# A two-layer decoder trunk on one core: the modulation rows' weights fetched one background step ahead of their sums

## The chip, the core and the metric

The kernel runs on one core of a Trainium2 chip. The core has a matrix engine (TensorE, in the profile PE, with its weight loads as PEld), VectorE (DVE), ScalarE (ACT), GpSimd (POOL) and SyncE (SP, which here only issues transfers). The engines run their own instruction streams and meet at semaphores. The metric is the device time of one execution in microseconds (us); a run's time is that of its slowest core, and there is one core here.

## What is computed

The reference is a trunk of two layers over a sequence of 512 tokens with 1024 channels. Each layer takes six modulation rows of 1024 numbers from the conditioning vector `c`, and uses them around a token mixer and a mixture of experts:

```python
ada_in = jax.nn.silu(c)
for i in range(DEPTH):
    mod = (ada_in @ w_ada[i] + b_ada[i]).reshape(b, 6, d)
    sh_m, sc_m, g_m = ...   # rows 0, 1, 2
    sh_f, sc_f, g_f = ...   # rows 3, 4, 5
    hm = rmsnorm(x, norm_mix[i]) * (1 + sc_m) + sh_m
    y = dilated_mixer(hm, ...) if i % 2 == 0 else forgetting_mixer(hm, ...)
    x = x + g_m * y
    hf = rmsnorm(x, norm_ffn[i]) * (1 + sc_f) + sh_f
    x = x + g_f * hierarchical_moe(hf, ...)
```

Layer 0 uses the dilated mixer ("mixer A": one projection to 9216 columns, three groups of attention with 16 heads each, merged by their denominators, and an out-projection). Layer 1 uses the forgetting mixer ("mixer B"). There are 16 experts per layer, all of them evaluated.

## The kernel before

The program is written in a tile framework: at build time a scheduler takes the operations in the order in which the code emits them, the free buffers of each pool and its own costs, and fixes from them one order of instructions for each engine. So a change of where the code emits something can move instructions on every engine.

**The background rows.** The first two rows of layer 0 are made at the start, in `begin`. The other ten are made by `ada` (L383 to L418), a generator of which `background` (L1324) makes ten, called jobs here. Each job needs 4 MB of weights, in eight pieces of 128 x 1024 numbers (512 KB): piece `kt` is fetched by SP into a tile of the tag `raw` (L393), and VectorE adds it to the accumulator with one scalar_tensor_tensor, `acc = piece * csil[kt] + acc` (L394; "a sum" below). Then the accumulator, which has 128 partial rows, is rounded to a high part `hi` on ScalarE (L399), a low part `nlo` is taken on VectorE (L400), and four TensorE matmuls with a column of ones add up the 128 partitions (L406 for the high part, L409 for the low). The row is evicted (L413 or L415) and stored (L416). There is one accumulator, one `nrow` and one `nlo`, so that the jobs follow one another.

**The weave.** `weave` (L227) runs the main work of mixer A and calls `next` on the front job once in two of its steps: a step of the main work is, for instance, a few projection matmuls. So the ten jobs are spread over mixer A, 12 calls to a job. The main work here is the projection (`part`, L295, L296 and L298: high times high, low times high, high times low) and attention: `qn`, the normed queries and keys, comes from VectorE (L470), is transposed on TensorE (L657, L658) and evicted into `qt` by ScalarE (L661) and into `kt` by VectorE (L662). The logits come from TensorE (L683 or L692), VectorE adds the bias (L691, the custom instruction), ScalarE takes the exponential (L693), TensorE transposes the result `nl` (L702), which VectorE or ScalarE evicts as `pt` (L209, L207), and L722 multiplies it with the values. `qn` and `nl` are transposed into banks of the same PSUM tag, so an eviction of `kt` also gives a bank back to L702.

**Buffers.** The tag `raw` has four buffers. The stream of projection weights (`Stream`, L107) holds up to three of them during mixer A, and the background job has what is left; the high part of its row (L398) sits there too. `row` has two buffers, which `nrow` and `nlo` hold during the jobs. When the last job is through, the row `g_m` of layer 0 is fetched into one of them (L606), and VectorE multiplies the weights of the out-projection with it (L149).

Of the kernel before, what the change touches and what calls it, by code (L numbers as in the profile page):

```python
# [20 lines left out]
KT = D // P  # L21
# [156 lines left out]
class Trunk:  # L178
# [205 lines left out]
    def ada(self, layer, j, norm, put):  # L384

        nc, i = self.nc, self.i
        acc = self.w.tile([P, D], F32, name="acc", tag="acc", bufs=1)
        row = self.nrow
        nc.gpsimd.memset(acc, 0.0)
        nc.gpsimd.dma_start(out=acc[0:1, :], in_=i["b_ada"][layer:layer + 1, j * D:(j + 1) * D])  # L390
        for kt in range(KT):
            raw = self.w.tile([P, 1024], F32, name="ada", tag="raw", bufs=4)
            nc.sync.dma_start(out=raw, in_=i["w_ada"][layer, kt * P:(kt + 1) * P, j * D:(j + 1) * D])  # L393
            nc.vector.scalar_tensor_tensor(acc, raw, self.csil[:, kt:kt + 1], acc, op0=OP.mult, op1=OP.add)  # L394
            if norm is not None and kt == KT // 2:
                nc.sync.dma_start(out=row, in_=self.bcast(norm, D, 1))
            yield
        hi, lo = self.w.tile([P, 1024], F32R, name="ada", tag="raw", bufs=4), self.nlo  # L398
        nc.scalar.activation(hi, acc, AF.Copy)  # L399
        nc.vector.tensor_tensor(lo, acc, hi.bitcast(F32), op=OP.subtract)  # L400
        for _ in range(3):
            yield
        ts = [self.bank("s")[0:1, :], self.bank("s")[0:1, :]]
        for h in range(2):
            cs = slice(h * 512, (h + 1) * 512)
            nc.tensor.matmul(ts[h], lhsT=self.one, rhs=hi[:, cs], start=True, stop=False)  # L406
        for h in range(2):
            cs = slice(h * 512, (h + 1) * 512)
            nc.tensor.matmul(ts[h], lhsT=self.one, rhs=lo[:, cs], start=False, stop=True)  # L409
        for h in range(2):  # L410
            cs = slice(h * 512, (h + 1) * 512)
            if norm is not None:
                nc.vector.scalar_tensor_tensor(row[:, cs], ts[h], 1.0, row[:, cs], op0=OP.add, op1=OP.mult)  # L413
            else:
                nc.scalar.activation(row[:, cs], ts[h], AF.Copy)  # L415
        nc.scalar.dma_start(out=put, in_=row)  # L416
        if (layer, j) == (0, 2):
            self.g_m = self.load_row(layer, 2)  # L418
# [986 lines left out]
```

## Time and profile before

| | us |
|---|---|
| median of 3 runs (1465.14, 1470.24, 1475.07) | 1470.24 |
| the profiled execution | 1476.0 |
| its span in the profile | 1474.2 |
| TensorE busy in it (matmuls) | 1328.8 (90%) |
| VectorE busy | 966.6 (66%) |
| ScalarE busy | 652.1 (44%) |
| the ten jobs' sums, L394, VectorE busy | 111.9 (80 instructions) |
| idle VectorE time just before them | 112.5 |

The profile gives busy times of each engine, a table of waits (which line of which engine stood idle, and whose work ended that), and the trace of single instructions with their start, length and, in brackets, the idle time ahead of each on its engine with what ended it. PEclk is the clock that TensorE was granted, as a share of its full 2.4 GHz.

### The profile page before, as it was taken

Reading aid. Unit: us, or ns where it says so; the run is one execution under the profiler, and the core shown is the slowest. Engines: PE = TensorE matmul, PEld = TensorE weight load, DVE = VectorE, ACT = ScalarE, POOL = GpSimd, SP = SyncE. Lnnn points to the kernel's source line nnn. Section 1 sums busy time; section 2 is a strip of 40 time slices with the busy share of each in tenths; the row PEclk is TensorE's granted clock in tenths of the full one; section 3 lists DMA queues with packets and bytes.
Section 4 is the critical chain, followed back from the end, with each engine's and each line's share of the span. In section 5 each row is a group of like instructions: output and inputs, shape, how many; then the busy total and the mean of one; then the engine's idle time right before and its main releaser. Section 6 shows DMA issues by size and latency. Waiting matters only on the chain. (4 is left out here: it accounts for less than half of the span.)

```text
span 1474.2 us, 20070 instructions
## 1 busy us (share of the span) xinstructions
PE 1328.8 (90%) x7017; PEld 1075.1 (73%) x7017; DVE 966.6 (66%) x1841; ACT 652.1 (44%) x1356; POOL 294.9 (20%) x192
## 2 busy tenths in 40 slices
PE   5799999989998999999969998499999999799995
PEld 3688888868986988887756665268888878566663
DVE  6775766675666675664677775376766753877772
ACT  6333544344433453344245554344544542355551
POOL 2312111221121211110232221211111100332221
PEclk9899999999999999999979999799999999889998
DMA  9356444644454645254679998604222463799981
GB/s 358 117 174 203 143 138 139 192 124 153 145 156 158 188 131 176 68 187 132 232 257 302 283 294 253 179 17 123 72 66 86 133 197 125 253 293 311 306 279 24
DMA packets 187156, 264.15 MB, mean 179 GB/s; under 512 B 23064, under 2 KB 148696, under 8 KB 187046
## 3 DMA queue, kind: packets, MB, share of 16 engines
q1 hardware_dynamic: 160742, 227.86, 47.5%
q0 software_dynamic: 8576, 16.85, 4.9%
q10 hardware_dynamic: 17728, 18.05, 4.1%
q8 instruction: 59, 0.97, 0.3%
q14 instruction: 51, 0.42, 0.1%
HBM read 249.85 MB, written 25.43 MB: 187 GB/s over the span
## 5 line engine op out<-in xcount | busy, mean ns | idle before, releaser
L295 PE MATMUL ps_pj<-hi,h 128*128 128x512 f32 (+1 forms) x1016 | 395.5, 398 | 6.2 <-ACT h L455 3.3
L296 PE MATMUL ps_pj<-lo,h 128*128 128x512 f32 (+1 forms) x1016 | 375.6, 378 | 0.8 <-POOL lo L153 0.8
L298 PE MATMUL ps_pj<-hi,h 128*128 128x512 f32 (+1 forms) x1016 | 290.0, 375 | 5.5 <-POOL h L380 5.4
L153 POOL TENSOR_TENSOR lo<-raw,hi 128x1024 fp32r<-128x1024 f32 x56 | 139.9, 2498 | 620.3 <-ACT hi L150 567.2
L295 PEld LDWEIGHTS ps_pj<-hi,h 128*128 128x128 f32 x1016 | 239.7, 236 | 31.5 <-issue 6.6
L296 PEld LDWEIGHTS ps_pj<-lo,h 128*128 128x128 f32 x1016 | 241.1, 237 | 16.6 <-POOL lo L153 1.4
L298 PEld LDWEIGHTS ps_pj<-hi,h 128*128 128x128 f32 x1016 | 212.1, 236 | 27.3 <-POOL h L380 7.8
L394 DVE SCALAR_TENSOR_TENSOR acc<-ada,csil,acc 128x1024 f32<-128x1024 f32 x80 | 111.9, 1399 | 112.5 <-DMA ada<-in_w_ada 112.2
L150 ACT ACTIVATE hi<-raw 128x1024 fp32r<-128x1024 f32 x126 | 132.2, 1051 | 100.0 <-PE ps_pj L298 52.1
L153 DVE TENSOR_TENSOR lo<-raw,hi 128x1024 fp32r<-128x1024 f32 x70 | 102.8, 1471 | 33.0 <-ACT hi L150 30.0
L295 PE MATMUL ps_pj<-hi,xh 128*112 128x512 f32 x256 | 105.4, 412 | 0.0
L296 PE MATMUL ps_pj<-lo,xh 128*112 128x512 f32 x256 | 104.0, 406 | 0.0
L298 PE MATMUL ps_pj<-hi,xl 128*112 128x512 f32 x256 | 80.9, 397 | 0.0
L1237 DVE SCALAR_TENSOR_TENSOR y<-ps_s,r_ws,g_f 112x512 f32<-112x512 f32 x64 | 47.9, 748 | 35.0 <-PE ps_s L1236 35.0
L455 ACT ACTIVATE xh<-ps_t 128x448 fp32r<-128x448 f32 x64 | 31.8, 542 | 84.3 <-PE ps_t L450 84.3
L462 ACT ACTIVATE sq<-ps_pj 128x512 f32<-128x512 f32 x63 | 37.0, 589 | 61.8 <-PE ps_pj L298 50.9
L927 DVE CUSTOM_DVE_ANT_0 nl<-ps_s,cums 128x128 f32<-128x128 f32 (+1 forms) x64 | 31.0, 484 | 46.5 <-PE ps_s L925 43.4
L153 DVE TENSOR_TENSOR lo<-h,hi 128x1024 fp32r<-128x1024 f32 x42 | 51.1, 1223 | 15.6 <-ACT hi L150 14.7
L722 PEld LDWEIGHTS ps_o<-vr,pt 128*128 128x128 f32 x480 | 58.0, 192 | 1.4
L929 ACT ACTIVATE nl<-nl,mn 128x128 f32<-128x128 f32 (+1 forms) x64 | 35.8, 559 | 50.6 <-DVE mn L927 50.0
L722 PE MATMUL ps_o<-vr,pt 128*128 128x64 f32 x480 | 57.3, 271 | 0.0
L464 DVE TENSOR_REDUCE qss<-sq 128x8 f32<-128x512 f32 x64 | 43.4, 679 | 20.0 <-ACT sq L462 19.7
(283 smaller groups left out, 2306.7 us busy)
## 6 DMA issues: line engine op xcount, KB each, us to landing
ada<-in_w_ada SPq DMA_DIRECT2D x85, 512.0 KB
raw<-in_a_w_in SPq DMA_DIRECT2D x128, 256.0 KB
h<-in_w_gate SPq DMA_DIRECT2D x42, 256.0 KB
h<-in_w_up SPq DMA_DIRECT2D x42, 256.0 KB
mix<-in_w_gate SPq DMA_DIRECT2D x37, 256.0 KB
mix<-in_w_up SPq DMA_DIRECT2D x37, 256.0 KB
raw<-in_w_down SPq DMA_DIRECT2D x18, 512.0 KB
h<-in_w_down SPq DMA_DIRECT2D x18, 512.0 KB
```

Source lines behind the costliest of these rows:

```text
L150: t.act = nc.scalar.activation(h, r, AF.Copy)
L153: eng.tensor_tensor(l, r, h.bitcast(F32), op=OP.subtract)
L295: nc.tensor.matmul(out, lhsT=hi, rhs=wh, start=first and n == 0, stop=False)
L296: nc.tensor.matmul(out, lhsT=hi, rhs=wl, start=False, stop=False)
L298: nc.tensor.matmul(out, lhsT=lo, rhs=wh, start=False, stop=last and n == len(terms) - 1)
L394: nc.vector.scalar_tensor_tensor(acc, raw, self.csil[:, kt:kt + 1], acc, op0=OP.mult, op1=OP.add)
L455: self.nc.scalar.activation(hv, tv, AF.Copy)
L462: nc.scalar.activation(sq, ps, AF.Square)
L464: nc.vector.tensor_reduce(ss, sq.rearrange("p (h d) -> p h d", d=HD), axis=AX.X, op=OP.add)
L722: nc.tensor.matmul(held["o"][:, at:at + HD], lhsT=pt[:, a * P:(a + 1) * P], rhs=v, start=(m == 0), stop=(m == len(terms) - 1))
L929: nc.scalar.activation(pr[:, sl], pr[:, sl], AF.Exp, scale=-1.0, bias=mn, accum_out=held["d"][:, h * 4 + b:h * 4 + b + 1])
L1237: nc.vector.scalar_tensor_tensor(y[:, cs], yp, m["ws"][0:CAP, e:e + 1], m["g_f"][0:CAP, cs], op0=OP.mult, op1=OP.mult)
```

## The change

The load of piece `kt + 1` is emitted right behind the sum of piece `kt`, ahead of the `yield`, and the first piece is fetched in a step of its own. A job then takes 13 calls of `next` in place of 12. No buffer is added, and each sum, cast and matmul is as before. In the changed kernel all lines from the load on have other numbers: the load is L394, the sum L401, the cast L408, the low part L409, the matmuls L415 and L418, and any line behind them is the old one plus 9 (L662 becomes L671, L691 L700, L149 stays).

```diff
--- before.py
+++ after.py
@@ -388,10 +388,19 @@
         row = self.nrow
         nc.gpsimd.memset(acc, 0.0)
         nc.gpsimd.dma_start(out=acc[0:1, :], in_=i["b_ada"][layer:layer + 1, j * D:(j + 1) * D])
-        for kt in range(KT):
+
+        def load(kt):
             raw = self.w.tile([P, 1024], F32, name="ada", tag="raw", bufs=4)
             nc.sync.dma_start(out=raw, in_=i["w_ada"][layer, kt * P:(kt + 1) * P, j * D:(j + 1) * D])
+            return raw
+
+
+        raw = load(0)
+        yield
+        for kt in range(KT):
             nc.vector.scalar_tensor_tensor(acc, raw, self.csil[:, kt:kt + 1], acc, op0=OP.mult, op1=OP.add)
+            if kt + 1 < KT:
+                raw = load(kt + 1)
             if norm is not None and kt == KT // 2:
                 nc.sync.dma_start(out=row, in_=self.bcast(norm, D, 1))
             yield
```

What the scheduler makes of it: the order on TensorE and VectorE is the same up to the end of the first job, and again from the end of mixer A's last projection to the end of the program. Between the two it differs on all engines. Three places follow. In these rows a wait is named by the semaphore of the engine or transfer queue that it waits on (DVE, Activation, PE, DMAHW); the number behind a tile's name is its number in the program.

**The fifth job.** SP in the kernel before, where the fifth job (accumulator `acc_2202`) fetches its last pieces:

```order
L114 DMA raw_2314<-in_a_w_in 128x4x256 [waits DMAHW3_49,DVE_49]
L114 DMA raw_2345<-in_a_w_in 128x2x256 [waits DMAHW4_49,DMAHW0_49,DVE_49]
L114 DMA raw_2345<-in_a_w_in 128x2x256 [waits DMAHW5_49]
L393 DMA ada_2348<-in_w_ada 128x1024 [waits DMAHW1_49,DVE_49]
L114 DMA raw_2361<-in_a_w_in 128x2x256 [waits DMAHW2_49,DVE_49]
L114 DMA raw_2361<-in_a_w_in 128x2x256
L114 DMA raw_2374<-in_a_w_in 128x2x256 [waits DMAHW3_49,Pool_49]
L114 DMA raw_2374<-in_a_w_in 128x2x256
L393 DMA ada_2377<-in_w_ada 128x1024 [waits DMAHW6_49,DVE_49]
```

SP in the changed kernel, the same job:

```order
L394 DMA ada_2364<-in_w_ada 128x1024 [waits DMAHW2_49,DVE_49]
L394 DMA ada_2385<-in_w_ada 128x1024 [waits DMAHW7_49,DMAHW0_49,DVE_49]
L394 DMA ada_2400<-in_w_ada 128x1024 [waits DMAHW1_49,DMAHW0_49,DVE_49]
L394 DMA ada_2455<-in_w_ada 128x1024 [waits DMAHW1_49,DVE_49]
L394 DMA ada_2470<-in_w_ada 128x1024 [waits DMAHW3_49,DMAHW2_49,DVE_49]
L114 DMA raw_2624<-in_a_w_in 128x2x256 [waits DMAHW4_49,DVE_49]
```

In both, a load of a piece waits for VectorE; the last five loads of this job, with weight loads among them before, now stand in a row. TensorE in the kernel before, around the same job's four matmuls (`ada_2398` is the high part):

```order
L657 MATMUL ps_t_2540<-J_417,qn_2449 128x128 [waits DVE_49,Activation_49]
L658 MATMUL ps_t_2540<-ident_87,qn_2449 128x128
L657 MATMUL ps_t_2540<-J_417,qn_2449 128x128
L406 MATMUL ps_s_2476<-ada_2398,one_99 1x512 [waits Activation_49]
L406 MATMUL ps_s_2477<-ada_2398,one_99 1x512
L658 MATMUL ps_t_2540<-ident_87,qn_2449 128x128
L295 MATMUL ps_pj_2533<-hi_2148,h_75 128x512
L296 MATMUL ps_pj_2533<-lo_2149,h_75 128x512
L295 MATMUL ps_pj_2533<-hi_2148,h_75 128x512
L409 MATMUL ps_s_2476<-nlo_443,one_99 1x512 [waits DVE_49]
L409 MATMUL ps_s_2477<-nlo_443,one_99 1x512
```

And in the changed kernel (`ada_2553` is the high part):

```order
L295 MATMUL ps_pj_2730<-hi_2356,h_79 128x256
L296 MATMUL ps_pj_2730<-lo_2357,h_79 128x256
L295 MATMUL ps_pj_2730<-hi_2356,h_79 128x256
L296 MATMUL ps_pj_2730<-lo_2357,h_79 128x256
L298 MATMUL ps_pj_2730<-hi_2356,h_78 128x256 x2
L298 MATMUL ps_pj_2730<-hi_2356,h_80 128x256 x2
L415 MATMUL ps_s_2762<-ada_2553,one_99 1x512 [waits PE_49]
L415 MATMUL ps_s_2763<-ada_2553,one_99 1x512 [waits DVE_49,PE_49]
L418 MATMUL ps_s_2762<-nlo_443,one_99 1x512
L418 MATMUL ps_s_2763<-nlo_443,one_99 1x512
```

Before, the first L406 waits for ScalarE's cast and stands between two transposes of `qn_2449`; now L415 stands behind the whole group of projection matmuls into `ps_pj_2730` and has no wait on ScalarE left.

**A `kt` in the eighth job.** VectorE in the kernel before, around one write of `kt` (L662) that gives a bank back to L702:

```order
L394 SCALAR_TENSOR_TENSOR acc_3922<-ada_4034,csil_109,acc_3922 128x1024 [waits DMAHW3_49]
L691 ISA nl_4088,st_3785<-ps_s_4074,bias_3783 128x256 [waits PE_49]
L691 ISA st_3785 128x1
L691 ISA nl_4088,st_3785<-ps_s_4074,bias_3783 128x256
L691 ISA st_3785 128x1
L464 TENSOR_REDUCE qss_4111<-sq_4109 128x8 [waits Activation_49]
L662 TENSOR_SCALAR kt_3752<-ps_t_4136,gains_419 128x2x128 [waits Activation_49]
```

And the write at the same place of the projection in the changed kernel (L671):

```order
L209 COPY pt_4042<-ps_t_4041 128x512 [waits PE_49]
L700 ISA nl_4058,st_3766<-ps_s_4048,bias_3764 128x256 [waits PE_49]
L700 ISA st_3766 128x1
L700 ISA nl_4058,st_3766<-ps_s_4048,bias_3764 128x256
L700 ISA st_3766 128x1
L700 ISA nl_4063,st_3766<-ps_s_4049,bias_3764 128x256 [waits PE_49]
L700 ISA st_3766 128x1
L700 ISA nl_4063,st_3766<-ps_s_4049,bias_3764 128x256
L700 ISA st_3766 128x1
L401 SCALAR_TENSOR_TENSOR acc_3722<-ada_4010,csil_109,acc_3722 128x1024 [waits DMAHW6_49,DVE_49]
L473 TENSOR_REDUCE qss_4084<-sq_4082 128x8 [waits Activation_49]
L671 TENSOR_SCALAR kt_3730<-ps_t_4109,gains_419 128x2x128 [waits Activation_49]
```

The sum stood ahead of the second pair of logits and now stands between the logits and `kt`, with one reduction between.

**The end of the last job.** VectorE in the kernel before, from the last `kt` of the projection on; the sums and `nlo` of the last job stand 22 rows and more ahead of this:

```order
L662 TENSOR_SCALAR kt_4314<-ps_t_5004,gains_419 128x2x128 [waits Activation_49]
L153 TENSOR_TENSOR lo_5039<-raw_4876,hi_5038 128x1024 [waits Activation_49]
L153 TENSOR_TENSOR lo_5082<-raw_4902,hi_5081 128x1024 [waits DMAHW3_49,Activation_49]
L149 TENSOR_TENSOR raw_5073<-raw_5073,row_1659 128x1024 [waits DMAHW2_49,DMAHW0_49,DVE_49]
L149 TENSOR_TENSOR raw_5085<-raw_5085,row_1659 128x1024 [waits DMAHW3_49,DMAHW1_49,Pool_49]
L149 TENSOR_TENSOR raw_5097<-raw_5097,row_1659 128x1024 [waits DMAHW4_49,DVE_49]
L149 TENSOR_TENSOR raw_5341<-raw_5341,row_1659 128x1024 [waits DMAHW5_49,DMAHW0_49,Pool_49]
L691 ISA nl_5143,st_5132<-ps_s_5133,bias_5130 128x256 [waits PE_49]
```

And in the changed kernel:

```order
L401 SCALAR_TENSOR_TENSOR acc_4801<-ada_4940,csil_109,acc_4801 128x1024 [waits DMAHW2_49,DVE_49]
L153 TENSOR_TENSOR lo_5027<-raw_4851,hi_5026 128x1024 [waits Activation_49]
L153 TENSOR_TENSOR lo_5073<-raw_4880,hi_5072 128x1024 [waits DMAHW4_49,Activation_49]
L401 SCALAR_TENSOR_TENSOR acc_4801<-ada_4962,csil_109,acc_4801 128x1024 [waits DMAHW3_49,DVE_49]
L401 SCALAR_TENSOR_TENSOR acc_4801<-ada_4977,csil_109,acc_4801 128x1024 [waits DMAHW4_49,DVE_49]
L401 SCALAR_TENSOR_TENSOR acc_4801<-ada_5002,csil_109,acc_4801 128x1024 [waits DMAHW5_49,DVE_49]
L409 TENSOR_TENSOR nlo_443<-acc_4801,ada_5063 128x1024 [waits Activation_49]
L700 ISA nl_5143,st_5132<-ps_s_5133,bias_5130 128x256 [waits PE_49]
L700 ISA st_5132 128x1
L700 ISA nl_5143,st_5132<-ps_s_5133,bias_5130 128x256
L700 ISA st_5132 128x1
L149 TENSOR_TENSOR raw_5061<-raw_5061,row_1781 128x1024 [waits DMAHW7_49,DMAHW3_49]
```

The last job's five last sums moved behind the merge of the attention groups, three of them into adjacent rows; L149 (which multiplies with the row that is fetched when this job is through) stood ahead of the logits of the block and now stands between them.

## Rows read from the trace of the kernel before

**Rows 1.** Busy times by stretch: busy us of each engine (instructions), clock, DMA share, GB/s.

```profile
65.00:660.00 595.00, 557.09 (x3085) 501.45 (x3083) 390.43 (x762) 249.22 (x609) 106.99 (x58) 0.97 0.49 153
257.60:261.00 3.40, 3.40 (x9) 1.88 (x10) 3.40 (x8) 2.43 (x4) 1.44 (x2) 0.50 0.62 175
261.00:264.40 3.40, 3.40 (x17) 3.33 (x16) 2.09 (x5) 1.73 (x4) 1.94 (x2) 0.99 0.90 272
459.00:462.40 3.40, 3.39 (x10) 2.71 (x11) 1.31 (x5) 0.90 (x3) 0.00 (x0) 0.50 0.80 243
520.50:523.90 3.40, 3.40 (x14) 2.60 (x15) 1.78 (x6) 0.83 (x4) 0.95 (x1) 0.51 0.52 174
```

**Rows 2.** Waits of TensorE, 65 to 660 us: line, waited for: us in total, times, longest.

```profile
PE ps_s L406 <- ACT ada L399: 20.3, 9, 3.7
PE ps_t L702 <- ACT nl L693: 4.6, 2, 2.5
PE ps_s L409 <- DVE nlo L400: 4.4, 4, 2.8
```

**Rows 3.** L406 and L409 one by one: start, us, what ran [idle before <- releaser].

```profile
200.48 0.62 PE L406 MATMUL ps_s<-ada,one 128*1 128x512 f32 x2 [1.75 <-ACT ada L399]
201.74 0.62 PE L409 MATMUL ps_s<-nlo,one 128*1 128x512 f32 x2 [0.64 <-DVE nlo L400]
257.58 1.01 PE L406 MATMUL ps_s<-ada,one 128*1 128x512 f32 x2 [3.04 <-ACT ada L399]
306.03 0.59 PE L406 MATMUL ps_s<-ada,one 128*1 128x512 f32 x1 [3.74 <-ACT ada L399]
359.92 0.95 PE L406 MATMUL ps_s<-ada,one 128*1 128x512 f32 x2 [1.92 <-ACT ada L399]
361.18 1.01 PE L409 MATMUL ps_s<-nlo,one 128*1 128x512 f32 x2 [0.31 <-DVE nlo L400]
465.30 0.63 PE L406 MATMUL ps_s<-ada,one 128*1 128x512 f32 x2 [2.57 <-ACT ada L399]
518.24 0.63 PE L406 MATMUL ps_s<-ada,one 128*1 128x512 f32 x2 [1.30 <-ACT ada L399]
519.50 0.63 PE L409 MATMUL ps_s<-nlo,one 128*1 128x512 f32 x2 [0.63 <-DVE nlo L400]
```

**Rows 4.** Groups of instructions: busy us, mean ns of one, idle before them and releaser.

```profile
L394 DVE SCALAR_TENSOR_TENSOR acc<-ada,csil,acc 128x1024 f32<-128x1024 f32 x80 | 111.9, 1399 | 112.5 <-DMA ada<-in_w_ada 112.2
L295 PE MATMUL ps_pj<-hi,h 128*128 128x512 f32 (+1 forms) x542 | 218.1, 409 | 0.0
```

**Rows 5.** Waits of SP's queue, whole span.

```profile
SPq L393 <- DMA ada<-in_w_ada: 141.2, 41, 5.3
```

**Rows 6.** One turn of load and sum, at 90 us, from the timeline.

```profile
89.84 5.21 SPq L393 DMA_DIRECT2D ada<-in_w_ada  x2
93.41 1.28 DVE L394 SCALAR_TENSOR_TENSOR acc<-ada,csil,acc 128x1024 f32<-128x1024 f32 x1 [0.71 <-DMA ada<-in_w_ada]
```

**Rows 7.** Timeline around 299 us: a sum ahead of the logits.

```profile
296.79 1.88 DVE L394 SCALAR_TENSOR_TENSOR acc<-ada,csil,acc 128x1024 f32<-128x1024 f32 x1 [2.82 <-DMA ada<-in_w_ada]
298.60 0.41 DVE L691 CUSTOM_DVE_ANT_0 nl<-ps_s,bias 128x256 f32<-128x256 f32 x1
299.70 0.44 PE L702 MATMUL ps_t<-ident,nl 128*128 128x128 f32 x2 [2.50 <-ACT nl L693]
```

**Rows 8.** Timeline, two more L702 behind a sum, at 388 and 459 us.

```profile
384.35 2.77 DVE L394 SCALAR_TENSOR_TENSOR acc<-ada,csil,acc 128x1024 f32<-128x1024 f32 x1 [1.34 <-DMA ada<-in_w_ada]
388.17 0.55 PE L702 MATMUL ps_t<-ident,nl 128*128 128x128 f32 x3 [0.63 <-DVE kt L662]
459.01 0.69 PE L702 MATMUL ps_t<-ident,nl 128*128 128x128 f32 x2 [2.06 <-ACT nl L693]
```

**Rows 9.** Timeline of the end of the last job.

```profile
578.84 0.33 ACTq L606 DMA_DIRECT2D row<-mods  x1
605.56 3.25 DVE L149 TENSOR_TENSOR raw<-raw,row 128x1024 f32<-128x1024 f32 x1
```

## The prediction

> **What bounds the kernel now.** I read the busy times of the stretch in which the ten jobs lie, then TensorE's waits in it, then the single waits, then VectorE's and SP's side of them. From 65 to 660 us TensorE is busy 557.1 of 595 us [rows 1], so all that any order of the same work can win there is 37.9 us, beside what the clock costs. Of these 37.9 us the jobs' own matmuls hold most: L406 waits 20.3 us for the cast and L409 4.4 us for the low part [rows 2], 24.7 us together. VectorE stands idle 112.5 us ahead of the 80 sums, nearly all of it for the piece to land [rows 4], yet it is busy only 390.4 of those 595 us [rows 1]: its waits cost time only where TensorE soon needs what stands behind the sum.
>
> Why a piece lands late is seen on SP: its queue stands 141.2 us at L393 until a piece has landed and been added [rows 5]. One turn shows it: a load starts at 89.84 us and the sum of that piece at 93.41 us, after 3.6 us, with 0.71 us of waiting [rows 6]. The load could not start before the sum ahead of it had given its buffer back, since the weight stream holds the other three.
>
> **The change part by part.** *The load ahead.* It takes the buffer that the sum just emitted frees, so its earliest start is the end of that sum, as before; the order of the fifth job shows each of its loads still waiting on VectorE. Of the 70 loads behind a job's first, the one that waits for the sum just ahead of it is the usual case in either kernel, and VectorE's work between two sums decides how much of a turn is covered. So the 112.5 us of VectorE's waits stay within some 15 us: the cover moves from place to place, and is not more. The Trainium skill (DMA: Bandwidth & Descriptors, section Rules for kernel authors) says to issue the transfer early and to wait for it late, so that its fixed cost overlaps. By that rule the piece would be there when its sum comes, and the time would be that of the first rival below; SP's wait of 141.2 us [rows 5] says that the issue is early on paper only. A second sentence of the Trainium skill speaks against this change (Perfetto Trace Analysis, section Optimization Strategy): a gap that repeats can mean that there isn't a buffer for the next tile; the 41 waits in that row agree.
>
> *The loads on SP.* The same 80 loads go out. In the fifth job five stand in a row, with weight loads behind them. Runs of five or six such loads are in the order of before as well, and L295 still has an idle time of 0.0 in this stretch [rows 4]: three raw pieces and the rounded ones behind them hide it. I cost it at nothing; without that cover a weight that is one turn late would cost 3.6 us plus a sum of 1.28 us [rows 6], 4.9 us each.
>
> *The thirteenth step.* Ten more calls spread the jobs over more of mixer A, and the last ends later. What it moves decides the sum, in six terms against the profiled 1476.0 us.
>
> (1) Waits that go. In the fifth, sixth, eighth and ninth jobs the four matmuls now stand behind work that waits for later VectorE results, and the order leaves L415 no wait on ScalarE (shown for the fifth). Their waits were 3.74, 1.92 and 0.31, 2.57, 1.30 and 0.63 [rows 3]: 10.5 us. In the third and fourth jobs a wait is still there, but several projection matmuls of some 0.4 us [rows 4] more stand ahead of it; 1.75, 0.64 and 3.04 [rows 3], 5.4 us, should go. Together -15.9 us; if the third and fourth stay, -10.5.
>
> (2) Waits that stay. The remaining 24.7 - 15.9 = 8.8 us belong to the first, second, seventh and tenth jobs. The first job's order is unchanged. In the other three the last sums stand closer to the matmuls; the tenth has three in adjacent rows, so that each pays its turn. Bounds: nothing more, or one turn of 4.9 us more each. I take 1.5 us for two of them and 3 us for the tenth: +6.
>
> (3) The clock. After five of the waits in (1) the granted clock falls to 0.50, the lower of TensorE's two levels (1.2 GHz), for one record of 3.4 us: the first at 257.6 us and the last at 520.5 us are shown. 9 matmuls run in 3.4 us at the low level and 17 in the next 3.4 us at full clock [rows 1], so a record costs up to half of it; I take 1.5 us. Five go, -7.5; two come back with the longer waits of (2), +3. Net -4.5 us.
>
> (4) Old waits behind a sum. VectorE works in order, so a sum that waits for its piece holds what stands behind it. At 296.79 us a sum starts 2.82 us late, the logits behind it start at 298.60, and L702 waits 2.50 us [rows 7]; at 388 us it is a `kt` and 0.63 us; at 459 us it is logits again and 2.06 us [rows 8], with a low-clock record behind it [rows 1]. Those places are reordered: -5.2 and -1.5 for the record, -6.7 us.
>
> (5) New waits behind a sum. In the changed order a sum stands directly ahead of a `kt` whose bank a transpose soon needs at seven places (one is shown, in the eighth job), where four stood so before. Each is bounded by 0.63 us below and by 3.74 us, the longest wait that a late job has caused [rows 3], above. The middle of these bounds is 2.2 us, near the two rows in which the sum itself stood waiting (2.50 and 2.06), so I take 2.3 us: +16. One of the three old waits had a record behind it, so two or three of the seven should, at 1.5 us: +4. Together +20 us.
>
> (6) The tail. L149 needs the row `g_m`, whose load went out at 578.84 us while L149 first ran at 605.56 [rows 9]: 26.7 us of cover. Now L149 stands a few rows behind the last job's low part and ahead of the second pair of logits, so the load is not covered, and the second pair waits behind it. Bounds: nothing if TensorE has projection work enough, 4.9 us (a load and a pass of VectorE like that of rows 6) if it has none. I take +3 us.
>
> Sum: -15.9 + 6 - 4.5 - 6.7 + 20 + 3 = +1.9 us, so 1477.9 us for an execution like the profiled one. That one lies 5.8 us above the median of the runs, so against the median I forecast 1470.24 + 1.9, about 1472 us. All terms at their good ends (second nothing, fifth 7 x 0.63 with one record, sixth nothing) give -15.9 - 7.5 - 6.7 + 5.9 = -24 us; with (5) at 3.74 and a record at each place, (1) at -10.5, (2) at 3 x 4.9, (6) at 4.9, they give +35 us, but that needs every place at its worst.
>
> **The rivals.**
>
> *A, the waits go and nothing follows.* The load is early enough, or the new places are covered: the 24.7 us of L406 and L409 go with seven records of low clock (10.5 us), -35 us; if only term (1) and its records go, -23 us. About 1435 to 1447 us. For it: VectorE has a third of this stretch free. Against it: the buffer is given back by the same sum as before, and seven sums stand ahead of a `kt`.
>
> *B, the swap that I forecast.* Waits move from the jobs' own matmuls to the transposes: -8 to +14 us, 1462 to 1484 us.
>
> *C, slower: VectorE's order becomes the wait.* At the seven `kt` places the sum's load started only at the sum before it, and each place costs nearly a whole turn, as L406 did at its worst: 3.74 us and a record. Then (5) is 7 x 5.2 = 37 us in place of 20, the sum about +19, 1489 us. It decides from about 4 us a place on. For it: in the row shown, sum, reduction and `kt` follow one another directly. Against it: the worst of the three old places cost 2.50 us, since TensorE had projection matmuls between.
>
> *D, the change does not do what it says.* No load is earlier, the jobs' matmuls meet their cast as late as before, and what moves on VectorE is hidden: 1467 to 1475 us.
>
> **How the numbers follow.** A measurement of this kernel can tell about 1% from no change, 14.7 us: under 1455.5 us is faster, above 1485 us slower. B gets 0.58, D 0.11, A 0.14, C 0.17. The predicted time is B's, 1472 us; its own range is 1462 to 1484. The range that leaves out not over 2 in 10 runs from 1455 us, into the weak half of A, to 1488 us, into the weak half of C. Faster by over 1%: 0.14 (A); slower: 0.17 (C); within 1%: 0.69 (B and D).
>
> **What would show it.** VectorE's idle time ahead of the sums, now at L401, should stay between 100 and 130 us. L415 and L418 should wait 8 to 18 us together, none of it in the fifth, sixth, eighth and ninth jobs. L711, the former L702, should wait 10 to 20 us behind `kt` (L671) and logits, where the three old places waited 5.2 [rows 7, 8]. L149 should show an idle time for its row. TensorE's idle time from 65 to 660 us should be within 10 us of 37.9, and the last job should end later than 578 us. I am wrong if the idle time at L401 falls below 80 us (the loads are early, A), if the L711 waits stay below 8 us (A), or exceed 25 us (C), or if L295 begins to wait, which no term holds.

## The result

The changed kernel takes 1481.74 us (median of 5 runs, 1479.65 to 1483.14) against 1471.53 us of the kernel before (5 runs): the ratio is 1.0064, 95% interval 1.0041 to 1.0086, so 10 us or 0.6% slower. The forecast was 1472 us with a range from 1455 to 1488, and "within 1%" was given 0.69. The two profiled executions, 1476.0 and 1479.88 us, differ by less than the medians: the first lies 4.5 us above its kernel's median, the second 1.9 us under. One of the six runs of e5_two_buffers_alone in the table below (1469.04 us) lies over 1.5% above the fastest of that kernel and is left out of its median and its ratio.

Busy times of the changed kernel by stretch (us busy of each engine, instructions in brackets, then the clock granted to TensorE, DMA share, GB/s); the row that answers to [rows 1] and one to the start of the out-projection:

```profile
65.00:660.00 595.00, 555.08 (x3023) 500.54 (x3022) 383.07 (x760) 244.73 (x603) 105.04 (x58) 0.96 0.49 152
65.00:665.30 600.30, 560.38 (x3069) 505.84 (x3068) 384.78 (x762) 246.77 (x606) 105.04 (x58) 0.96 0.49 151
```

and the same stretch, to the start of its out-projection, of the kernel before:

```profile
65.00:658.10 593.10, 555.19 (x3069) 500.12 (x3068) 390.43 (x762) 247.59 (x606) 106.49 (x57) 0.97 0.49 153
```

The same 3069 matmuls take 600.30 us where they took 593.10, so 7.2 us are lost here, and they split in two: TensorE idles 600.30 - 560.38 = 39.9 us in place of 37.9, 2.0 us more, and is busy 5.2 us longer with the same work, because its clock was lower (0.96 in place of 0.97 by these rows; the units are counted below). In the rest of the kernel, which is the same code, the two profiled executions differ by 3.4 us the other way (spans 1478.0 and 1474.2), so the profiles assign 7.2 us of the loss to the changed stretch; they are one execution of each kernel, and 3.4 us is what two executions of the same code differ by here. The mean granted clock is on record for every run of the experiments: the span times one minus this clock is 78.5 us in the changed kernel (median of 5 runs) and 69.0 to 70.6 us in the kernel before (63 runs in three sessions). Since a low clock costs nothing while TensorE idles, this bounds the clock's part: at most 8 to 9.5 of the 10 us.

TensorE's waits in the changed kernel, 65 to 690 us (line, waited for, us in total, times, longest), which answer to [rows 2]:

```profile
PE ps_s L415 <- ACT ada L408: 13.1, 3, 6.1
PE ps_t L711 <- DVE kt L671: 13.0, 5, 3.7
PE ps_t L666 <- DVE qn L479: 5.6, 3, 2.3
PE ps_t L666 <- ACT hi L150: 2.8, 1, 2.8
PE ps_t L711 <- ACT pt L207: 2.5, 2, 1.5
PE ps_t L666 <- DVE kt L671: 1.5, 1, 1.5
PE ps_s L418 <- DVE nlo L409: 1.1, 3, 0.5
```

The jobs' own matmuls wait 14.2 us (L415 and L418) where they waited 24.7, and the transposes wait 13.0 us for `kt`; of these 1.77 us, at 654 us, are a wait of before that lies behind the last job (1.86 us there), and 11.2 us are new, where the three old places had 5.2. Single waits of the changed kernel, as in [rows 3] and [rows 8] (start, length, what ran, idle time ahead of it):

```profile
152.75 1.01 PE L415 MATMUL ps_s<-ada,one 128*1 128x512 f32 x2 [3.49 <-ACT ada L408]
309.18 0.66 PE L711 MATMUL ps_t<-ident,nl 128*128 128x128 f32 x4 [1.62 <-DVE kt L671]
324.06 0.90 PE L711 MATMUL ps_t<-ident,nl 128*128 128x128 f32 x3 [3.72 <-DVE kt L671]
446.12 0.87 PE L415 MATMUL ps_s<-ada,one 128*1 128x512 f32 x2 [3.49 <-ACT ada L408]
494.48 0.90 PE L711 MATMUL ps_t<-ident,nl 128*128 128x128 f32 x3 [3.71 <-DVE kt L671]
545.10 0.74 PE L711 MATMUL ps_t<-ident,nl 128*128 128x128 f32 x3 [2.19 <-DVE kt L671]
612.61 1.01 PE L415 MATMUL ps_s<-ada,one 128*1 128x512 f32 x2 [6.11 <-ACT ada L408]
```

Groups of instructions of the changed kernel (busy, mean ns, idle time ahead and what ended it), as in [rows 4], with SP's wait, as in [rows 5]:

```profile
L401 DVE SCALAR_TENSOR_TENSOR acc<-ada,csil,acc 128x1024 f32<-128x1024 f32 x80 | 109.0, 1363 | 111.1 <-DMA ada<-in_w_ada 108.7 <-DMA acc<-in_b_ada 1.6 <-issue 0.4
L295 PE MATMUL ps_pj<-hi,h 128*128 128x512 f32 (+1 forms) x548 | 220.1, 407 | 0.0
SPq L394 <- DMA ada<-in_w_ada: 149.7, 45, 5.9
```

VectorE's idle time ahead of the sums is 111.1 us after 112.5, and SP's wait 149.7 after 141.2: no load is earlier. That L295 group has no idle time, so the weights behind the row of loads on SP were not late.

### The profile page after: what moved, and what is told of

It reads as the page before. It is cut to its first block, busy times and chain, and to the rows that moved or that the text cites. A ratio compares the mean times of both kernels' runs of the same rounds, so it can differ in the third digit from the quotient of the medians.

```text
span 1478.0 us, 20055 instructions
## 1 busy us (share of the span) xinstructions
PE 1331.4 (90%) x7017; PEld 1080.0 (73%) x7017; DVE 959.1 (65%) x1841; ACT 651.4 (44%) x1356; POOL 293.7 (20%) x192
## 5 line engine op out<-in xcount | busy, mean ns | idle before, releaser
L295 PE MATMUL ps_pj<-hi,h 128*128 128x512 f32 (+1 forms) x1016 | 396.1, 398 | 6.6 <-ACT h L464 3.9
L296 PE MATMUL ps_pj<-lo,h 128*128 128x512 f32 (+1 forms) x1016 | 376.2, 378 | 1.5 <-POOL lo L153 1.4
L295 PEld LDWEIGHTS ps_pj<-hi,h 128*128 128x128 f32 x1016 | 241.3, 238 | 31.7 <-issue 6.7
L296 PEld LDWEIGHTS ps_pj<-lo,h 128*128 128x128 f32 x1016 | 242.3, 238 | 17.8 <-POOL lo L153 1.8
L401 DVE SCALAR_TENSOR_TENSOR acc<-ada,csil,acc 128x1024 f32<-128x1024 f32 x80 | 109.0, 1363 | 111.1 <-DMA ada<-in_w_ada 108.7
L153 DVE TENSOR_TENSOR lo<-raw,hi 128x1024 fp32r<-128x1024 f32 x70 | 97.2, 1391 | 30.5 <-ACT hi L150 27.3
L295 PE MATMUL ps_pj<-hi,xh 128*112 128x512 f32 x256 | 105.7, 413 | 3.0 <-ACT xh L464 3.0
L296 PE MATMUL ps_pj<-lo,xh 128*112 128x512 f32 x256 | 104.5, 408 | 0.0
L295 PEld LDWEIGHTS ps_pj<-hi,xh 128*112 128x112 f32 x256 | 45.9, 179 | 16.7 <-ACT xh L464 3.9
```

The lines of the kernel that those rows point to most:

```text
L153: eng.tensor_tensor(l, r, h.bitcast(F32), op=OP.subtract)
L295: nc.tensor.matmul(out, lhsT=hi, rhs=wh, start=first and n == 0, stop=False)
L296: nc.tensor.matmul(out, lhsT=hi, rhs=wl, start=False, stop=False)
```

## The experiments

Each median stands beside its ratio to the kernel before, which ran on the same chip between the runs of the experiment (1472.3, 1472.1 and 1472.1 us in the three sessions). "Calls" are the calls of `next` of one job.

| kernel | calls | load | buffers of the jobs | us | ratio (95%) |
|---|---|---|---|---|---|
| before | 12 | beside its sum | 1 | 1472 | 1 |
| changed | 13 | a step ahead | 1 | 1481.7 | 1.0064 (1.0041 to 1.0086) |
| e1_step_only | 13 | beside | 1 | 1480.1 | 1.0053 (1.0032 to 1.0074) |
| e2_load_only | 12 | a step ahead | 1 | 1458.5 | 0.9900 (0.9865 to 0.9935) |
| e3_step_later | 13 | beside | 1 | 1481.8 | 1.0057 (1.0036 to 1.0077) |
| e4_two_buffers | 13 | a step ahead | 2 | 1443.3 | 0.9809 (0.9775 to 0.9844) |
| e5_two_buffers_alone | 12 | beside | 2 | 1453.1 | 0.9859 (0.9820 to 0.9899) |
| e6_load_two_buffers | 12 | a step ahead | 2 | 1454.5 | 0.9874 (0.9841 to 0.9906) |
| e7_eleven_steps | 11 | beside | 1 | 1477.9 | 1.0045 (1.0019 to 1.0072) |
| e8_one_load | 12 | first piece only | 1 | 1436.2 | 0.9761 (0.9724 to 0.9798) |
| e9_step_later_two | 13 | beside | 2 | 1451.0 | 0.9870 (0.9843 to 0.9896) |
| e10_after_kt_act | 13 | a step ahead | 1 | 1474.7 | 1.0027 (1.0005 to 1.0049) |
| e11_before_kt_act | 12 | beside | 1 | 1467.7 | 0.9973 (0.9954 to 0.9993) |
| e12_three_buffers | 13 | a step ahead | 3 | 1447.1 | 0.9845 (0.9818 to 0.9872) |

**The change taken apart: the step.** The step alone, ahead of the first piece:

```diff
         nc.gpsimd.dma_start(out=acc[0:1, :], in_=i["b_ada"]...)
+        yield
         for kt in range(KT):
```

> Only the thirteenth step of the change: a bare step ahead of each job's first piece; the load stands beside its sum again. Theory: what the change costs (10 us, 1481.7 against 1471.5) comes from the extra step, which moves all jobs against the projection in the order, so 5 to 20 us over the kernel before, with L702 waiting 10 us or more behind kt and the jobs' matmuls 10 to 18 us. Rival 1, the place of the load costs (SP stands in it with weight loads behind): then this kernel is within 4 us of the kernel before.

1480.1 us, within 2 us of the changed kernel, so the first rival is out. The single waits are not those expected: up to 690 us its transposes wait 9.4 us for `kt` (10 or more expected) and the jobs' matmuls 18.4 us for the cast (10 to 18 expected). Then the step put behind the cast, ahead of the four matmuls:

```diff
-        for _ in range(3):
+        for _ in range(4):
             yield
```

> The kernel before with the thirteenth step put elsewhere: four empty steps in place of three between the cast and the four matmuls; loads as before. Its order on TensorE is nearly that of the changed kernel, that of VectorE is not. Theory (the extra step's shift on TensorE decides): 1475 to 1485 us, with the jobs' matmuls waiting 10 to 18 us and L702 behind kt 8 to 14 us. Rival: if the shift is harmless and where the sums stand on VectorE decides, then it is 1472 us or less and the kt waits stay under 5 us.

1481.8 us, the changed kernel's time. TensorE's waits of this kernel, 65 to 640 us:

```profile
PE ps_s L406 <- ACT ada L399: 13.5, 4, 6.0
PE ps_t L702 <- DVE kt L662: 13.0, 5, 5.5
```

They are near those of the changed kernel in the same window (13.1 us for the cast, 11.2 for `kt`), and the built orders tell why: on SP the two programs have the same rows in the same order, on VectorE the 80 sums stand at the same distances from one another, and on TensorE the orders differ in some 30 of 4200 rows. In the changed kernel the load of piece `kt` is emitted in call `kt`, just as here; what moved is the sum, to a call later, and the scheduler puts the sum where its piece is due in either case. So after scheduling the change is one more empty step ahead of the four matmuls, and next to nothing else. My expectation held here; that the sums' places on VectorE would come out the same I had not foreseen.

**The load.** The load ahead without the step:

```diff
-        raw = load(0)
-        yield
+        raw = load(0)
         for kt in range(KT):
```

> Only the load of the change: each piece is emitted right behind the sum ahead of it, with no extra step, so 12 calls a job. Theory: the place of the load alone costs nothing, since it waits for the same buffer as before; the time is at or under the kernel before (1450 to 1475 us), with VectorE's idle time ahead of the sums still 95 to 125 us. Rival 1, the load's place costs: 1478 us or more. A third way, that a load emitted early is early on the chip: the idle time ahead of the sums falls under 80 us.

1458.5 us, 14 us under the kernel before. Now each load but the first is emitted a call earlier than before, counted from the start of its job; against the job's four matmuls the distance is that of the changed kernel, and the job is a call shorter. Groups and waits of this kernel:

```profile
L400 DVE SCALAR_TENSOR_TENSOR acc<-ada,csil,acc 128x1024 f32<-128x1024 f32 x80 | 108.3, 1354 | 88.2 <-DMA ada<-in_w_ada 84.9 <-issue 1.2 <-DMA acc<-in_b_ada 1.2
```

```profile
PE ps_s L414 <- ACT ada L407: 11.2, 4, 4.8
PE ps_t L710 <- DVE kt L670: 9.8, 5, 2.2
```

The sums' idle time falls to 88.2 us, below the expected 95 to 125 and above the 80 that would have spoken for loads that are really early; the jobs' matmuls wait 11.2 us for the cast in place of 20.3, and the `kt` waits rise as well, to 9.8. So the time lies in the range that I gave, but "costs nothing" is not all: with the job's length kept at 12 calls, loads one call earlier gain 14 us. The first rival (the place of the load costs) is out. From this kernel to the changed one only the step is added, and it costs 23 us. Whether the earlier loads gain by themselves, or by another place of the sums that happens to fall well, this run does not separate.

**The number of steps.** Eleven calls:

```diff
-        for _ in range(3):
+        for _ in range(2):
             yield
```

> The kernel before with 11 calls a job: two empty steps in place of three between the cast and the four matmuls. Theory A, a step more is a cost by itself (jobs end later): a step less gains, 1468 us or less. Theory B, what a number of steps costs depends on where it puts the sums and matmuls against the projection, and 12 falls well: 1475 to 1485 us, with waits of L702 behind kt of 8 us or more, as with 13.

1477.9 us, 6 us slower than twelve. With 11 and with 13 calls the kernel is slower, so a step more is not a cost by itself (theory A falls). Its profiled execution took 1469.8 us, less than the median of the kernel before, so the waits in it, though they are those expected, do not account for the 6 us:

```profile
PE ps_s L406 <- ACT ada L399: 15.2, 6, 5.9
PE ps_t L702 <- DVE kt L662: 9.8, 3, 4.3
PE ps_t L702 <- DVE rs_y L219: 3.9, 1, 3.9
```

In the order of before, the fourth, seventh and tenth jobs have the same distances between their sums on VectorE, and their L406 stand some 160 us apart (257.6, 415.9 and 576.1 us): three jobs go with one quarter of the projection. With 11 or 13 calls they drift against it. That the drift as such costs, and not the particular places, was not tested. By the mean clocks of all runs, 73.8 us are lost to the clock with 11 calls and 69.0 with 12 in the same session.

**The buffer.** The changed kernel, with two of the four `raw` buffers for the weight stream in place of three, so that a job holds two:

```diff
-        elif self.held["raw"] < (4 if self.moe else 3):
+        elif self.held["raw"] < (4 if self.moe else 2):
```

> The changed kernel, but the weight stream may hold only two of the four raw buffers during mixer A, so that the jobs have two and the load of a piece no longer waits for the sum ahead of it. Theory (the load is early on paper only, for want of a buffer): VectorE's idle time ahead of the sums falls from 109 us to 75 or less, the jobs' matmuls wait under 6 us, the time falls under 1465 us, unless the weights, with one buffer less, come late (then L295 or L298 shows waits in the trace). Rival 2, VectorE's waits for the pieces cost nothing: 1476 to 1486 us.

1443.3 us, 38 us under the changed kernel and 29 under the one before: the fastest kernel of this study that computes the whole. The sums' group, TensorE's largest waits and the stretch from 65 to 660 us:

```profile
L401 DVE SCALAR_TENSOR_TENSOR acc<-ada,csil,acc 128x1024 f32<-128x1024 f32 x80 | 110.7, 1384 | 67.6 <-DMA ada<-in_w_ada 66.9 <-issue 0.3
```

```profile
PE ps_t L666 <- DVE qn L479: 11.4, 7, 2.6
PE ps_t L711 <- DVE kt L671: 1.8, 1, 1.8
```

```profile
65.00:660.00 595.00, 573.89 (x3248) 518.81 (x3248) 397.86 (x809) 261.69 (x652) 109.30 (x60) 0.98 0.52 162
```

The jobs' matmuls no longer appear among the waits, L711 waits 1.8 us for `kt`, TensorE does 3248 matmuls in 595 us where it did 3085 and 3023. SP's wait at the load's line falls from 149.7 to 55.2 us, so the loads do go out without waiting for the sum ahead. The weights, with one buffer less, bring one new wait of 0.7 us at L296. The second rival (the waits for the pieces cost nothing) is out. The Trainium skill (Perfetto Trace Analysis, section Optimization Strategy) says that a gap which repeats on the engine that should be saturated can mean too little room for the next tile. Here the gap is on VectorE, which is not that engine, and its fall from 111.1 to 67.6 us with one buffer more is this case's measure of it.

The same buffer without the change:

> The kernel before with the buffer alone: the weight stream holds two raw buffers in mixer A and the jobs two, each load emitted beside its sum as before, 12 calls a job. Theory: the buffer, not the place of the load in the code, decides; 1440 to 1458 us, with VectorE's idle time ahead of the sums at 60 to 85 us and the jobs' matmuls waiting under 10 us. Rival, the load has to be emitted a step ahead as well: 1465 us or more and an idle time over 95 us.

```profile
L394 DVE SCALAR_TENSOR_TENSOR acc<-ada,csil,acc 128x1024 f32<-128x1024 f32 x80 | 108.5, 1357 | 81.5 <-DMA ada<-in_w_ada 77.7 <-DMA acc<-in_b_ada 3.3
```

1453.1 us and an idle time of 81.5 us, as expected: the buffer alone gains 19 us, so it acts where the load stands beside its sum. L406 waits 10.1 us, 6.6 of it for the cast, where under 10 was expected; the profiled execution took 1465.7 us, 13 us over the median. Then the load ahead, no step, and the buffer:

> The load emitted behind the sum ahead of it, no thirteenth step, two buffers for the jobs: the change without its step and with the buffer that it lacks. Theory: the two gains (14 us for the load without the step, 29 us for the buffer with the step) overlap, since both take away the same waits; the step's own cost is gone: 1430 to 1444 us, VectorE's idle time ahead of the sums under 65 us. Rival, the step costs nothing once the buffer is there: 1443 us as with it, within 3 us.

1454.5 us, a miss: I had expected 1430 to 1444, the two gains without the step's cost. The rival (the step costs nothing once the buffer is there) is out too: with two buffers and the load ahead, twelve calls take 11 us more than thirteen, where with one buffer they took 23 us less. So the sign of the step is not fixed. Of the kernels that load all pieces VectorE waits least here (58.5 us), and yet TensorE waits elsewhere (the profiled execution took 1458.9 us, that of e4_two_buffers 1440.1):

```profile
L400 DVE SCALAR_TENSOR_TENSOR acc<-ada,csil,acc 128x1024 f32<-128x1024 f32 x80 | 111.6, 1394 | 58.5 <-DMA ada<-in_w_ada 56.8 <-DMA acc<-in_b_ada 1.3
```

```profile
PE ps_t L665 <- DVE qn L478: 11.0, 5, 3.0
PE ps_s L414 <- DVE st L699: 8.2, 2, 4.3
PE ps_s L691 <- DVE nrow L421: 2.3, 1, 2.3
```

The jobs' matmuls stand behind logits that VectorE has not read (8.2 us), the transposes wait for `qn` (11.0). The idle time of VectorE alone is not the measure of the time. Next, the step behind the cast with two buffers:

> The kernel before with four empty steps ahead of the matmuls in place of three (as in e3_step_later) and two buffers for the jobs, each load beside its sum. Its built order is nearly that of e4_two_buffers, in which the load is emitted a step ahead. Theory: the place of the load in the code is nothing even where a second buffer is there, so 1439 to 1449 us, like e4_two_buffers (1443.3). Rival, with the buffer the load ahead begins to count: 1452 us or more, like e5_two_buffers_alone.

1451.0 us, above the 1439 to 1449 of the theory and under the 1452 of the rival. Its interval (0.9843 to 0.9896) and that of e4_two_buffers (0.9775 to 0.9844) just touch, with nearly the same built order. Whether the load ahead gives some us once the buffer is there stays open.

One more buffer for the jobs, taken from the stream (`else 1`):

> e4_two_buffers with one raw buffer for the weight stream and three for the jobs in mixer A. Theory: e8_one_load gives the floor of what the waits for the pieces can return (1436 us), e4_two_buffers has 1443; a third buffer takes VectorE's idle time ahead of the sums from 68 to 40 to 60 us and the time to 1434 to 1444 us. Rival, the weights come late: L295 or L296 waits, 1450 us or more.

1447.1 us, outside the 1434 to 1444 that I expected, with the sums' idle time at 64.1 us, hardly lower than with two:

```profile
L401 DVE SCALAR_TENSOR_TENSOR acc<-ada,csil,acc 128x1024 f32<-128x1024 f32 x80 | 108.9, 1361 | 64.1 <-DMA ada<-in_w_ada 63.4 <-issue 0.4
```

No L296 waits, so the weights are not late; a third buffer gained nothing here.

**The floor.** Each job fetches its first piece and adds it eight times:

```diff
-            raw = self.w.tile(...)
-            nc.sync.dma_start(out=raw, in_=i["w_ada"][layer, kt * P:...])
+            if kt == 0:
+                raw = self.w.tile(...)
+                nc.sync.dma_start(out=raw, in_=i["w_ada"][layer, kt * P:...])
             nc.vector.scalar_tensor_tensor(acc, raw, ...)
```

> The price of all the waiting: each job fetches its first piece alone and adds it eight times (seven of the eight loads are left out, the sums stay, so the rows' values are others). Theory: VectorE's waits for the pieces cause nearly all of TensorE's waits in this stretch and most of the low-clock records: idle time ahead of the sums under 30 us, TensorE idle from 65 us to the end of the projections under 15 us, 1420 to 1440 us. Rival, the waits are hidden anyway: 1460 us or more.

```profile
L395 DVE SCALAR_TENSOR_TENSOR acc<-ada,csil,acc 128x1024 f32<-128x1024 f32 x80 | 111.7, 1397 | 14.4 <-DMA ada<-in_w_ada 13.7
```

```profile
65.00:660.00 595.00, 582.19 (x3274) 524.49 (x3273) 400.19 (x810) 266.49 (x653) 115.25 (x60) 0.99 0.33 102
```

1436.2 us. With the waits for the pieces nearly gone (14.4 us), TensorE idles 595 - 582.2 = 12.8 us in place of 37.9. So a kernel without 70 of the 80 loads, in an order of its own, is 36 us faster than the one before; the changed kernel with the second buffer is 29 us faster. The time and the idle times are as expected; that most of the low-clock records would go is not shown: of 16.1 us of clock lost between 65 and 640 us (counted as in the next section), 8.5 remain.

**The `kt` on another engine.** To see whether `kt` behind a sum is a cause and not only a mark, its eviction moves to ScalarE, in the changed kernel and as a control in the one before:

```diff
-                nc.vector.tensor_scalar(kt[:, :, c], tv[:, 2:4, :], g[:, 1:2], None, op0=OP.mult)
+                nc.scalar.activation(kt[:, :, c], tv[:, 2:4, :], AF.Copy, scale=g[:, 1:2])
```

> The changed kernel with the eviction of kt moved from VectorE to ScalarE (the 48 L671), so that no sum can stand ahead of it; the order on TensorE and SP stays nearly as it is. Theory, a kt held behind a sum is the new wait: the 13.0 us that L711 waited for kt and their low-clock records fall by more than half, and the time to 1462 to 1475 us. Rival, the transposes would have waited anyway (for qn, or for ScalarE in its own order): 1476 us or more, with as much waiting under another name.

> The control: the kernel before with the same move of kt to ScalarE. Theory: two waits of 2.5 us in all are what it can win beside what VectorE's lighter queue gives the jobs' matmuls; 1458 to 1472 us, so that the changed kernel gains more from the move than this one does. If both gain the same, the move helps for another reason, and it proves nothing on the kt.

1474.7 and 1467.7 us: 7.0 us under the changed kernel, 4.4 under the one before. The waits of the two, 65 to 640 us, first the changed kernel's:

```profile
PE ps_t L666 <- DVE qn L479: 14.6, 8, 3.3
PE ps_t L711 <- ACT kt L671: 7.9, 6, 3.7
```

```profile
PE ps_t L657 <- DVE qn L470: 8.9, 8, 2.7
PE ps_t L702 <- ACT kt L662: 0.9, 2, 0.6
```

In this window the wait for `kt` falls from 11.2 to 7.9 us, less than by half, and the wait for `qn` grows from 5.6 to 14.6, by more than that. At 343 us, for instance, `qn` stands behind a sum that waited 5.89 us for its piece. The profiled execution of the changed kernel with the move took 1486.2 us, 11.5 us over its median, so part of this can be that one execution. The times lie in the ranges of the theory, but by the ratios the changed kernel gains 0.37% and the kernel before 0.27%, and each ratio is uncertain by 0.2%, so this pair does not settle it. The trace, in the next section, shows at single places what `kt` waited behind; what it costs in all stays open.

## Why the prediction was right, and where it was off

*The load is no earlier.* Right: 111.1 us of idle time ahead of the sums, SP's wait a little longer, and the built order nearly the same as with a bare step behind the cast. The sentence of the Trainium skill (DMA: Bandwidth & Descriptors, section Rules for kernel authors) on issuing early is not contradicted by it: e2_load_only and e4_two_buffers, in which the loads do go out earlier, gain 14 and 29 us. In the changed kernel the issue itself was not early.

*(1) Waits that go: -15.9 us.* Right. In the third to sixth, eighth and ninth jobs no L415 waits; an L418 wait of 0.53 us stayed in the fourth.

*(2) Waits that stay: 8.8 + 6 us.* Right: 3.49, 3.49 and 6.11 us at L415 in the second, seventh and tenth jobs, 14.2 us with L418. The tenth, with its three adjacent sums, grew by 3.1 us as taken.

*(4) and (5), behind a sum: -5.2 and +16 us.* Right in kind at two places, and high in size. The old places are gone. New waits for `kt` are four, 1.62, 3.72, 3.71 and 2.19 us, 11.2 us in all in place of 7 x 2.3; but only at 309 and 494 us (5.3 us together) does a sum that waited stand ahead of `kt`, with one reduction between. The second of these is the eighth job's place whose order stands ahead of the prediction; from the changed kernel's timeline:

```profile
491.11 0.46 ACT L670 ACTIVATE qt<-ps_t,gains 128x256 f32<-128x256 f32 x1
492.15 1.28 DVE L401 SCALAR_TENSOR_TENSOR acc<-ada,csil,acc 128x1024 f32<-128x1024 f32 x1 [2.79 <-DMA ada<-in_w_ada]
493.95 0.47 DVE L671 TENSOR_SCALAR kt<-ps_t,gains 128x256 f32<-128x256 f32 x1
494.48 0.90 PE L711 MATMUL ps_t<-ident,nl 128*128 128x128 f32 x3 [3.71 <-DVE kt L671]
```

ScalarE has evicted its half of the bank by 491.57 us; the sum starts 2.79 us late, at 492.15, `kt` follows at 493.95, and the transposes start 3.71 us late. At the other two places (5.9 us) something else stands directly ahead of `kt`, which no term held:

```profile
320.53 2.54 POOL L153 TENSOR_TENSOR lo<-raw,hi 128x1024 fp32r<-128x1024 f32 x1 [32.76 <-ACT hi L150]
320.78 3.20 DVE L474 TENSOR_SCALAR qss<-qss 128x8 f32<-128x8 f32 x1
323.01 0.97 DVE L671 TENSOR_SCALAR kt<-ps_t,gains 128x256 f32<-128x256 f32 x1
542.28 2.35 POOL L153 TENSOR_TENSOR lo<-raw,hi 128x1024 fp32r<-128x1024 f32 x1 [7.43 <-ACT hi L150]
542.35 2.31 DVE L474 TENSOR_SCALAR qss<-qss 128x8 f32<-128x8 f32 x1
544.57 0.47 DVE L671 TENSOR_SCALAR kt<-ps_t,gains 128x256 f32<-128x256 f32 x1
```

L474, a VectorE instruction on 128 x 8 numbers that takes 0.16 us at 494 us, takes 3.20 and 2.31 us beside a pass of GpSimd, and `kt` starts within 0.06 us of that pass's end (323.06 and 544.63 us). At 324 us a sum (at 316.72, 1.84 us late) and the fifth job's low part stand farther ahead; at 545 us seven rows stand between the last sum, which had waited 0.47 us, and `kt`. The sums of [rows 7, 8] at 296.79 and 384.35 us, which ran 1.88 and 2.77 us in place of the 1.28 of [rows 6], lay beside such passes too, so the price that the prediction took from them was not of waits for a piece alone. No run here moves the GpSimd passes, so their share of the 10 us is open. Besides, the transposes wait 2.5 us for `pt`, 1.5 us for `kt` at 77 us (where the two orders are still the same) and 2.8 us at 419 us, which no term held either.

*(6) The tail: +3 us.* Wrong in the end, though L149 waits as said: the row's load went out at 616.24 us, and L149 stood idle for it,

```profile
616.24 0.33 ACTq L615 DMA_DIRECT2D row<-mods  x1
621.05 1.22 DVE L149 TENSOR_TENSOR raw<-raw,row 128x1024 f32<-128x1024 f32 x1 [1.83 <-DMA row<-mods]
```

1.83 us, but TensorE had projection work, as the lower bound said: no L692 waits more than 0.2 us.

So the waits sum to +2.0 us measured, where the terms gave -15.9 + 6 - 5.2 + 16 + 3 = +3.9. The nearness is partly luck: (4) and (5) were 4.8 us too high and (6) 3 us, and the 6.8 us that no term held made up for it.

*(3), and the records in (4) and (5): the clock, -2 us.* This is the term that failed: the same matmuls took 5.2 us longer. I had counted the records that go and guessed those that come, -4.5 - 1.5 + 4. Read through in windows of 1 us, the clock lost between 65 and 640 us, as the window times one minus the granted clock, is 16.1 us before and 22.2 us after, in units of 1.7 us, not of 1.5. Where the change took five units away, it brought more: one of L415's waits, that at 152 us, has three records behind it, which stayed at the lower level while TensorE was busy again all the time:

```profile
155.40:158.80 3.40, 3.40 (x18) 3.40 (x18) 0.00 (x0) 0.29 (x1) 0.37 (x1) 0.50 0.43 142
158.80:162.20 3.40, 3.40 (x23) 2.85 (x22) 0.82 (x2) 0.60 (x1) 0.00 (x0) 0.50 0.00 0
```

and the waits at 324 and 612 us have two records each. Of the seven waits listed under the result none was without one (the wait of 2.30 us for `qn` at 301 us was). So each of these seven waits, of 1.6 to 6 us, came with one to three units of 1.7 us, which cost time as far as TensorE was busy in them. That is no fixed price: in the kernel before, waits of 2.28 us at 150 us, 2.50 at 299 and 2.80 at 419 had none. Why the one at 152 us had three is open.

The sum (+1.9 us) thus had its waits right to 2 us, in part by errors that cancel, and its clock wrong by 7, where most of the loss in the profile came from; the forecast of no change beyond 1% held, with the median 10 us above the 1472 forecast.

*The rivals.* A, that the waits go and nothing follows, did not come true; its time was reached only with a buffer more (e4_two_buffers, 1443 us, inside A's 1435 to 1447). C, a whole turn at each place, was right for the length of two waits (3.7 us with records), of which one was a turn behind a sum, and wrong on their number. D, that the change does not do what it says, is true of the load, and the step still moved time.

## What to carry to other kernels

A prefetch in the code need not be one on the chip: look at what the load's semaphore waits for before counting on it, and give it a second buffer first (here taken from a stream that hardly missed it: 29 us gained with the change, 19 without). With one buffer the load ahead lost 10 us at 13 calls a job and gained 14 at 12. Where a scheduler sets the order, emitting a load or a yield elsewhere shifts everything around it; compare the built orders, since two edits that read quite differently can be the same program. Price a wait on a busy TensorE together with the low-clock records at it, not by its length alone. And before a wait is put down to the instruction ahead, read the length of each instruction between against its usual length.

## What was not expected of the hardware

The granted clock stayed at 0.50 for 10 us after one wait of 3.49 us (153 to 163 us in the changed kernel), through 6.8 us in which TensorE was busy without a gap, while waits of like length elsewhere had 3.4 us of it (446 and 494 us) or 6.8 (324 us). In the profiled execution of the changed kernel with `kt` on ScalarE, the one of 1486.2 us, 10.2 us of clock were lost in one stretch from 608 to 628 us, around the tenth job's wait. And of the small VectorE instructions L474 and L217 to L219 of the changed kernel, which mostly take 0.17 us, thirteen took 0.96 to 3.20 us between 65 and 640 us; each overlapped a GpSimd pass, and twelve ended within 0.03 us of that pass's end. No run here tells why.
